# A hybrid RWKV-7 / HGRN2 layer: the input stage issued in the order of the first tile's parts, and the constants cleared by another engine

## The chip, the cores and the metric

The kernel runs on one core of one Trainium2 chip. The metric is the device time of one execution in microseconds (us), as a median of runs. The core has five engines that run side by side and meet through semaphores: TensorE (PE; its weight loads are listed apart as PEld), VectorE (DVE), ScalarE (ACT), GpSimd (POOL) and SyncE (SP), which here issues nearly all DMAs. Each engine works through its own instructions in the order in which they were issued.

## The reference

One decoder layer for two groups of tokens: 256 new tokens of one prompt, and 8 sequences of 8 tokens that continue from a stored state, 320 tokens together, D_MODEL = 2048. All is float32.

```
h = rms_norm(x, norm_g)
p = einsum('nld,dp->nlp', h, w_in)              # 2048 x 11392, one projection for everything
cur = p[..., :SHIFT_W]                          # r, k, v (1024 each), wd, ad (64 each)
sh = cur + (prev - cur) * shift_mu              # prev: the token before
w_log = -softplus(-(w0 + tanh(wd) @ w2)) - 0.5  # low-rank decay
a     = sigmoid(a0 + ad @ a2)                   # low-rank gate
y_a   = RWKV-7 recurrence, 16 heads of 64, group norm, bonus, times silu(za)
y_b   = HGRN2 recurrence, 8 heads of 128, norm, times silu(zb)
merged = sigmoid(ga) * (y_a @ proj_a) + sigmoid(gb) * (y_b @ proj_b)
y = rms_norm(x + merged @ w_out, final_norm_g)
```

The outputs are y for both groups and the new states.

## The kernel before

**Products in three parts.** A float32 operand is split in two rounded halves: `hi` (a ScalarE copy that rounds) and `lo` (the rest, by a subtraction on VectorE or GpSimd). A product is then three TensorE products, hi x hi, hi x lo and lo x hi. So a weight block of 1024 x 128 goes through four steps: a DMA of 512 KB into one of three buffers `wraw`, a copy into `whi` (ScalarE), a subtraction into `wlo`, and 24 TensorE products of 128x128 with 320 tokens. A tile of 128 output columns is two blocks. Block n uses buffer (n + 2) modulo 3.

**The input stage (lines 354 to 633).** The tokens are in three groups j: 0 and 1 are the prompt (128 tokens each), 2 is the sample (64). For each, `squares` and `scale` (ScalarE) give 1/rms, `gain` (VectorE) multiplies by it and by `norm_g` spread over all partitions (`gb`, made by four TensorE products of `sel` and `gr`, `gr` being the split `norm_g`), `turn` transposes on TensorE, `high` (ScalarE) and `low` (VectorE) split into `hhi` and `hlo`. Meanwhile `divide` splits the two blocks of the very first tile, the columns `wd` and `ad` (buffers 0 and 1), with GpSimd for the subtraction, and `first(k4)` issues its products, twelve for each quarter of the depth, all three parts of a quarter together. `warm(n)` issues n products of no use in between. Before all that GpSimd builds masks (lines 388 to 472); behind its last subtractions it clears constants (`jr_*`, `yz`, `qz`, `arp`, `lora_lw`, `lora_la`, `rs_a`, `rs_b`; lines 612 to 633). In this stage the order on each engine is the order of the program.

**The recorded stage (`record_all`, line 1318).** For eight heads, eight tiles each, then four tiles more, together with the two recurrences of a head (`rwkv`, `hgrn`). All operations are recorded first (`Recorder`); `order()` then plans them with a price for each operation, every engine free at time 0 of the plan, and issues them in the planned order: all of them therefore have the line 1376. TensorE's products of the big projection are filler: whatever else is ready goes between them. A tile's blocks are fetched in the plan too, from the third block on; the first two (buffers 2 and 0) are fetched and split in the input stage.

The first recorded work is `wd_ad`: it shifts the first tile's result (`shifted`, through `pad` and `dif`), takes tanh of its half `wd`, and puts both halves, split, into `lora_w`/`lora_lw` and `lora_a`/`lora_la`. Each is needed on both halves of the partitions, so the rounded one is copied over by GpSimd: `G.tensor_copy(dst[other], dst[own])`, line 1316. TensorE multiplies it with `wst` and `ast`, the split low-rank weights `w2a2` of the head. `bounds` computes small constants (`neg`, `lbt`).

**After it:** the gates ga and gb and the two projections (lines 1400 to 1421), then the output projection and the final norm (to line 1514).

Of the kernel before, what the change touches and what calls it, by code (L numbers as in the profile page):

```python
# [9 lines left out]
F32 = mybir.dt.float32  # L10
# [58 lines left out]
class Recorder:  # L69
# [118 lines left out]
    def order(self):  # L188

        self.link()  # L190
        free = dict.fromkeys(self.real, 0.0)
        ready = {e: [] for e in self.real}
        for o in self.ops:
            o.ready = 0.0
# [78 lines left out]
def hybrid_step(ctx, tc, x_prompt, x_sample, state_rwkv, state_hgrn, state_shift, norm_g, w_in,  # L273
# [80 lines left out]
    with tc.tile_pool(name="start", bufs=1) as st, \  # L354
# [21 lines left out]
        def divide(b_, n, sub):  # L376
            for j in range(n):
                ks = slice(8 * j // n, 8 * (j + 1) // n)
                S.copy(whi[b_][:, ks], wraw[b_][:, ks])
                sub.tensor_sub(wlo[b_][:, ks], wraw[b_][:, ks], whi[b_][:, ks].bitcast(F32))  # L380
            return whi[b_], wlo[b_]
# [95 lines left out]
        def squares(j, hf=None):  # L477
            xt, n = xts[j]
            cs = slice(0, D) if hf is None else slice(1024 * hf, 1024 * hf + 1024)
            S.activation(junk[:n, cs], xt[:n, cs], AF.Square, accum_out=ssq[j][:n, hf or 0:(hf or 0) + 1])  # L480

        def scale(j):
            n = xts[j][1]
            t_ = ssq[j][:n, 0:1]
            S.activation(t_, t_, AF.Ln, scale=1.0 / D, bias=eps_n[:n])
            S.activation(t_, t_, AF.Exp, scale=-0.5)

        def gain(j, k4, w=1):
            xt, n = xts[j]
            cs = slice(512 * k4, 512 * (k4 + w))  # L490
            V.scalar_tensor_tensor(xt[:n, cs], xt[:n, cs], ssq[j][:n, 0:1], gb[:n, cs], op0=ALU.mult, op1=ALU.mult)
# [13 lines left out]
        def high(j, k4):  # L505
            _, ks, tok = span(j, k4)
            S.copy(hhi[:, ks, tok], tps[j, k4])
# [8 lines left out]

        def warm(n):
            for _ in range(n):
                T.matmul(wps[:, :256], sel[:, 0], gr[:, :256], start=True, stop=True)

        tps = {}
        with tc.manual_schedule(engines={mybir.EngineType.PE, mybir.EngineType.Activation, mybir.EngineType.DVE,
                                        mybir.EngineType.Pool}):

            S.copy(gr[0:4], gq)
            V.tensor_sub(gr[32:36], gq, gr[0:4].bitcast(F32))
            for c_ in range(4):
                ps = pst.tile([128, 512], F32, name="gps", tag="t")
                T.matmul(ps, sel[:, c_], gr, start=True, stop=True)
                V.tensor_copy(gb[:, 512 * c_:512 * c_ + 512], ps)  # L530
            squares(2)
            scale(2)
            gain(2, 0, 2)
            turn(2, 0)
            warm(3)
            gain(2, 2, 2)
            turn(2, 1)
            warm(3)
            squares(0)
            scale(0)  # L540
            gain(0, 0, 2)
            turn(0, 0)
            turn(0, 1)
            warm(4)
            gain(0, 2, 2)
            squares(1, 0)
            squares(1, 1)
            V.tensor_add(ssq[1][:, 0:1], ssq[1][:, 0:1], ssq[1][:, 1:2])
            scale(1)
            gain(1, 0)  # L550
            turn(1, 0)
            warm(4)
            high(2, 0)
            high(0, 0)
            low(2, 0)
            low(0, 0)
            pre = [divide(0, 2, G)]
            first_ps = psm.tile([128, 512], F32, name="mps", tag="m")

            def first(k4):  # L560

                hi, lo = pre[k4 // 2]
                for w, x, last in ((hi, hhi, False), (hi, hlo, False), (lo, hhi, k4 == 3)):
                    for k_ in range(4 * k4, 4 * k4 + 4):
                        T.matmul(first_ps[:, :NT], w[:, k_ % 8], x[:, k_], start=w is hi and x is hhi and k_ == 0,
                                 stop=last and k_ == KT - 1)

            gain(1, 1)
            turn(1, 1)
            high(1, 0)  # L570
            low(1, 0)
            first(0)
            high(2, 1)
            high(0, 1)
            high(1, 1)
            gain(1, 2)
            low(2, 1)
            low(0, 1)
            low(1, 1)
            turn(0, 2)  # L580
            turn(1, 2)
            pre.append(divide(1, 2, G))
            gain(1, 3)
            first(1)
            for j in range(2):
                high(j, 2)
                low(j, 2)
            turn(0, 3)
            turn(1, 3)
            divide(2, 1, G)  # L590
            fetch(0, 0, 1)
            first(2)
            for j in range(2):
                high(j, 3)
                low(j, 3)
            ps = pst.tile([128, 512], F32, name="cps", tag="t")
            T.transpose(ps[:, :128], rows, ident)
            V.tensor_copy(cols, ps[:, :106])
            ps = pst.tile([128, 512], F32, name="sps", tag="t")
            for j in range(2):  # L600
                T.transpose(ps[:, 100 * j:100 * j + 100], ssr[:, j], ident[:100, :100])
            V.tensor_copy(sst.rearrange("p s r -> p (s r)"), ps[:, :200])
            first(3)
            divide(0, 1, G)
            for j in range(3):
                S.copy(seq4[32 * j:32 * j + 32], seqm[0:32, 0:4])
            S.copy(lvz[HS[1], :, 1], lvs[low_])
            S.copy(lvz[low_, :, 0], lvs[low_])

            jr_sum, jr_mean, jr_cent, jr_all = (ctile([128, 128], n, F32R)  # L610
                                                for n in ("jr_sum", "jr_mean", "jr_cent", "jr_all"))
            G.memset(jr_all.bitcast(F32), 1.0 / 128.0)
            for t_, x in ((jr_sum, 1.0), (jr_mean, 1.0 / 64.0)):
                G.memset(t_.bitcast(F32), 0.0)
                for sl in HS:
                    G.memset(t_[sl, sl].bitcast(F32), x)
            G.tensor_sub(jr_cent, ident, jr_mean.bitcast(F32))

            yz = ctile([128, 2, 2, 2, 64], "yz")
            yd = ctile([128, 2, 2, 64], "yd")  # L620
            qz = ctile([128, NSEQ, 32], "qz")
            arp = ctile([128, 5, 2, 2, 64], "arp")
            for t_ in (yz, qz, arp, lora_lw[HS[1]].bitcast(F32), lora_la[HS[0]].bitcast(F32)):
                G.memset(t_, 0.0)


            rs_a = ctile([128, NT], "rs_a")
            rs_b = ctile([128, NT], "rs_b")
            G.memset(rs_a, 1.0)
            G.memset(rs_a[:, 0:NP_:64], 0.0)  # L630
            G.memset(rs_a[:, NP_::8], 0.0)
            G.memset(rs_b, 1.0)
            G.memset(rs_b[:, ::8], 0.0)

    neg = ctile([128, 16], "neg")
    lbt = ctile([128, 4, 8], "lbt")
# [667 lines left out]
    def wd_ad(ps):  # L1304
        lsh = at("lsh", tag="uQ")
        shifted(24, lsh, ps)

        lo, hi = HS
        S.activation(lsh[lo], lsh[lo], AF.Exp, scale=2.0)
        S.activation(lsh[lo], lsh[lo], AF.Ln, bias=1.0)  # L1310
        S.activation(lsh[lo], lsh[lo], AF.Exp, scale=-1.0)
        V.tensor_scalar(lsh[lo], lsh[lo], -2.0, 1.0, op0=ALU.mult, op1=ALU.add)
        for dst, low, own, other in ((lora_w, lora_lw, lo, hi), (lora_a, lora_la, hi, lo)):
            S.copy(dst[own], lsh[own])
            V.tensor_sub(low[own], lsh[own], dst[own].bitcast(F32))
            G.tensor_copy(dst[other], dst[own])

    def record_all():
        io = {}
# [3 lines left out]
        def tile_of(c0, post):  # L1323
            ps = mps[ra["n"] // 2 % 2][:, :NT]
            for k8 in range(2):
                b_ = (ra["n"] + 2) % 3
                book.block = ra["n"]
                ra["n"] += 1
                raw, hi, lo = wraw[b_], whi[b_], wlo[b_]
                if ra["n"] > 2:  # L1330
                    Y.dma_start(raw, win[1024 * k8:1024 * k8 + 1024, c0:c0 + 128].rearrange("(k p) c -> p k c", p=128))
                    S.copy(hi, raw)
                    V.tensor_sub(lo, raw, hi.bitcast(F32))
                for q in range(8):
                    k = 8 * k8 + q
                    T.matmul(ps, hi[:, q, :], hhi[:, k, :], start=k == 0, stop=False)
                    T.matmul(ps, hi[:, q, :], hlo[:, k, :], start=False, stop=False)
                    T.matmul(ps, lo[:, q, :], hhi[:, k, :], start=False, stop=k == KT - 1)
            book.block = None
            post(ps)  # L1340
# [202 lines left out]
```

## Time and profile before

| | |
|---|---|
| median of 3 runs | 1167.26 us (1166.31 to 1167.61) |
| the profiled execution | 1170.25 us, its span 1168.5 us |
| TensorE busy | 1141.9 us, 98% of the span |
| VectorE busy | 777.8 us, 67% |
| ScalarE busy | 666.7 us, 57% |
| GpSimd busy | 210.6 us, 18% |
| DMA | 159.68 MB, mean 137 GB/s |

The span runs from the first to the last instruction in the trace. Busy time counts the instructions on an engine, whether they are of use or not. The page also cuts the span in 40 slices; GpSimd is busy in eight tenths of the first and in two to five tenths of those behind it, and DMA moves 168 GB/s in the first. A row of the order of time gives the start, the duration, the engine, the line, the operation, its output and inputs, and in brackets how long the engine stood idle before it and what ended the wait. A wait is put down to the last of its semaphores.

### The profile page before, as it was taken

Reading aid. Unit: us, or ns where it says so; the run is one execution under the profiler, and the core shown is the slowest. Engines: PE = TensorE matmul, PEld = TensorE weight load, DVE = VectorE, ACT = ScalarE, POOL = GpSimd, SP = SyncE. Lnnn points to the kernel's source line nnn. Section 1 sums busy time; section 2 is a strip of 40 time slices with the busy share of each in tenths; the row PEclk is TensorE's granted clock in tenths of the full one; section 3 lists DMA queues with packets and bytes.
Section 4 is the critical chain, followed back from the end, with each engine's and each line's share of the span. In section 5 each row is a group of like instructions: output and inputs, shape, how many; then the busy total and the mean of one; then the engine's idle time right before and its main releaser. Section 6 shows DMA issues by size and latency. Waiting matters only on the chain.

```text
span 1168.5 us, 20702 instructions
## 1 busy us (share of the span) xinstructions
PE 1141.9 (98%) x7775; PEld 1100.5 (94%) x7775; DVE 777.8 (67%) x1617; ACT 666.7 (57%) x1478; POOL 210.6 (18%) x429
## 2 busy tenths in 40 slices
PE   7899999999999999999999999999999999999996
PEld 6899999999999999999999999999999999988875
DVE  6778778877878888879788686444444434434542
ACT  6556766766666676667567667444444444433431
POOL 8532132122222221421321310000000000000000
PEclk9899999999999999999999999999999999999998
DMA  5643544434535435426435434555555555575632
GB/s 168 176 116 100 154 123 115 132 109 130 145 95 147 113 93 145 131 80 168 125 101 151 122 102 134 147 156 148 146 154 152 145 148 157 145 257 158 186 103 90
DMA packets 283831, 159.68 MB, mean 137 GB/s; under 512 B 22989, under 2 KB 273360, under 8 KB 283092
## 3 DMA queue, kind: packets, MB, share of 16 engines
q1 hardware_dynamic: 283220, 154.70, 47.1%
q0 software_dynamic: 512, 3.67, 1.0%
q8 instruction: 61, 1.00, 0.4%
q14 instruction: 38, 0.31, 0.1%
HBM read 148.53 MB, written 9.81 MB: 136 GB/s over the span
## 4 chain that ended last, share of the span: by engine, by line
PE 92%; DVE 3%; DMA 2%; ACT 1%; POOL 1%; issue 0%; DVEq 0%; SPq 0%; POOLq 0%; ACTq 0%
PE mps L1376 40%; PE a L1376 12%; PE mps L338 6%; PE mps L337 6%; PE mps L339 6%; PE b L1376 4%; PE po L1458 2%; PE po L1456 2%; PE po L1457 2%; DMA raw<-in_w_out_dram 2%; PE ppb L338 2%; PE ppa L338 2%; PE ppb L337 2%; PE ppa L337 2%; PE ppb L339 2%; PE ppa L339 2%
## 5 line engine op out<-in xcount | busy, mean ns | idle before, releaser
L1376 PE MATMUL mps<-hlo,whi 128*128 128x320 f32 x1088 | 345.4, 317 | 0.0
L1376 PE MATMUL mps<-hhi,whi 128*128 128x320 f32 x1088 | 345.3, 317 | 0.0
L1376 PE MATMUL mps<-hhi,wlo 128*128 128x320 f32 x1088 | 345.1, 317 | 0.0
L1376 PEld LDWEIGHTS mps<-hlo,whi 128*128 128x128 f32 x1088 | 205.4, 189 | 3.3 <-issue 3.0
L1376 PEld LDWEIGHTS mps<-hhi,wlo 128*128 128x128 f32 x1088 | 205.5, 189 | 2.7 <-issue 2.4
L1376 PEld LDWEIGHTS mps<-hhi,whi 128*128 128x128 f32 x1088 | 205.5, 189 | 0.8 <-issue 0.4
L328 DVE TENSOR_TENSOR wlo<-raw,whi 128x1024 fp32r<-128x1024 f32 x88 | 107.8, 1225 | 124.7 <-ACT whi L327 124.5
L327 ACT CAST whi<-raw 128x1024 fp32r<-128x1024 f32 x88 | 92.3, 1048 | 163.3 <-PE mps L338 107.4
L1376 ACT CAST whi<-raw 128x1024 fp32r<-128x1024 f32 x134 | 140.6, 1050 | 77.3 <-PE mps L1376 73.6
L1376 DVE TENSOR_TENSOR wlo<-raw,whi 128x1024 fp32r<-128x1024 f32 x134 | 166.7, 1244 | 24.7 <-ACT whi L1376 23.5
L337 PE MATMUL mps<-hhi,whi 128*128 128x320 f32 x448 | 138.4, 309 | 0.0
L338 PE MATMUL mps<-hlo,whi 128*128 128x320 f32 x448 | 138.4, 309 | 0.0
L339 PE MATMUL mps<-hhi,wlo 128*128 128x320 f32 x448 | 138.4, 309 | 0.0
L337 PEld LDWEIGHTS mps<-hhi,whi 128*128 128x128 f32 x448 | 84.1, 188 | 0.0
L338 PEld LDWEIGHTS mps<-hlo,whi 128*128 128x128 f32 x448 | 84.1, 188 | 0.0
L339 PEld LDWEIGHTS mps<-hhi,wlo 128*128 128x128 f32 x448 | 84.1, 188 | 0.0
L1449 DVE TENSOR_TENSOR wlo<-raw,whi 128x1024 fp32r<-128x1024 f32 x32 | 39.0, 1224 | 45.6 <-ACT whi L1448 45.5
L1448 ACT CAST whi<-raw 128x1024 fp32r<-128x1024 f32 x32 | 33.6, 1051 | 55.9 <-DMA raw<-in_w_out_dram 28.6
L1431 POOL DMA_DIRECT2D xb<-in_x_sample_dram x1 | 0.7, 721 | 341.7 <-PE mps L339 341.7
L1456 PE MATMUL po<-whi,mhi 128*128 128x512 f32 x128 | 50.7, 396 | 1.9 <-ACT whi L1448 1.2
L1458 PE MATMUL po<-wlo,mhi 128*128 128x512 f32 x128 | 50.8, 397 | 0.6 <-DVE wlo L1449 0.5
L1457 PE MATMUL po<-whi,mlo 128*128 128x512 f32 x128 | 50.5, 394 | 0.0
(410 smaller groups left out, 2344.0 us busy)
## 6 DMA issues: line engine op xcount, KB each, us to landing
raw<-in_w_in_dram SPq DMA_DIRECT2D x194, 512.0 KB
raw<-in_w_out_dram SPq DMA_DIRECT2D x32, 512.0 KB
raw<-in_proj_a_dram SPq DMA_DIRECT2D x16, 512.0 KB
raw<-in_proj_b_dram SPq DMA_DIRECT2D x16, 512.0 KB
s<-in_state_hgrn_dram SPq DMA_DIRECT2D x8, 512.0 KB
out_dram<-s SPq DMA_DIRECT2D x8, 512.0 KB
s<-in_state_rwkv_dram SPq DMA_DIRECT2D x8, 256.0 KB
out_dram<-s SPq DMA_DIRECT2D x8, 256.0 KB
```

Source lines behind the costliest of these rows:

```text
L327: S.copy(hi[:, ks], raw[:, ks])
L328: sub.tensor_sub(lo[:, ks], raw[:, ks], hi[:, ks].bitcast(F32))
L337: T.matmul(dst, hi[:, q, :], xhi[:, k, :], start=(k == 0), stop=False)
L338: T.matmul(dst, hi[:, q, :], xlo[:, k, :], start=False, stop=False)
L339: T.matmul(dst, lo[:, q, :], xhi[:, k, :], start=False, stop=(k == nk - 1))
L1376: o.fn(*o.args, **o.kw)
L1431: G.dma_start(yx[j], src)
L1448: S.copy(hi, raw)
L1449: V.tensor_sub(lo, raw, hi.bitcast(F32))
L1456: T.matmul(pt, h, hi, start=first, stop=False)
L1457: T.matmul(pt, l, hi, start=False, stop=False)
L1458: T.matmul(pt, h, lo, start=False, stop=end)
```

## The change

- **Constants.** The clears of lines 612 to 633 go from GpSimd to VectorE, to the very front of the stage, ahead of the split of `gr`; `arp` comes behind the copies of `gb`. A tile of ones, 128 x 256, is new.
- **Warming.** `warm` multiplies ones (128 partitions) instead of `sel` and `gr` (64 partitions). 16 such products are issued ahead of the first transposes; of those in between, 3 and 4 stay (before 3, 3, 4 and 4).
- **Order.** The products of the first tile are issued part by part: `first(part, k4)`, as soon as the operands of that part are there. The splits of its blocks are issued in halves (`half`) between the copies of `high`. The squares of group 1 are one instruction instead of two and an addition.
- **Second tile.** Its two blocks (buffers 1 and 2) are fetched in the input stage; the plan then begins to fetch with the fifth block.
- **Low-rank copies.** The copy to the other half of the partitions is a second ScalarE copy from `lsh` instead of one on GpSimd.
- **Plan.** The planner takes GpSimd as free from 1.7 us of the plan on.

```diff
         free = dict.fromkeys(self.real, 0.0)
+        free["G"] = 1700.0
...
         def warm(n):
             for _ in range(n):
-                T.matmul(wps[:, :256], sel[:, 0], gr[:, :256], start=True, stop=True)
+                T.matmul(wps[:, :256], ones[:, :128], ones, start=True, stop=True)
...
+            ones = st.tile([128, 256], F32R, name="ones")
+            V.memset(ones.bitcast(F32), 1.0)
+            V.memset(jr_all.bitcast(F32), 1.0 / 128.0)
+            for t_, x in ((jr_sum, 1.0), (jr_mean, 1.0 / 64.0)):
+                V.memset(t_.bitcast(F32), 0.0)
+                for sl in HS:
+                    V.memset(t_[sl, sl].bitcast(F32), x)
+            V.tensor_sub(jr_cent, ident, jr_mean.bitcast(F32))
...
+            for t_ in (yz, qz, lora_lw[HS[1]].bitcast(F32), lora_la[HS[0]].bitcast(F32)):
+                V.memset(t_, 0.0)
...
+            V.memset(rs_a, 1.0)
+            V.memset(rs_a[:, 0:NP_:64], 0.0)
+            V.memset(rs_a[:, NP_::8], 0.0)
+            V.memset(rs_b, 1.0)
+            V.memset(rs_b[:, ::8], 0.0)
             S.copy(gr[0:4], gq)
             V.tensor_sub(gr[32:36], gq, gr[0:4].bitcast(F32))
...
+            V.memset(arp, 0.0)
+            warm(16)
             squares(2)
...
-            squares(1, 0)
-            squares(1, 1)
-            V.tensor_add(ssq[1][:, 0:1], ssq[1][:, 0:1], ssq[1][:, 1:2])
+            squares(1)
...
-            pre = [divide(0, 2, G)]
...
-            def first(k4):
-                hi, lo = pre[k4 // 2]
-                for w, x, last in ((hi, hhi, False), (hi, hlo, False), (lo, hhi, k4 == 3)):
-                    for k_ in range(4 * k4, 4 * k4 + 4):
-                        T.matmul(first_ps[:, :NT], w[:, k_ % 8], x[:, k_], start=w is hi and x is hhi and k_ == 0,
-                                 stop=last and k_ == KT - 1)
+            def first(part, k4):
+                w, x = ((whi, hhi), (whi, hlo), (wlo, hhi))[part]
+                for k_ in range(4 * k4, 4 * k4 + 4):
+                    T.matmul(first_ps[:, :NT], w[k4 // 2][:, k_ % 8], x[:, k_], start=part == 0 and k_ == 0,
+                             stop=part == 2 and k_ == KT - 1)
+            def half(b_, hf):
+                ks = slice(4 * hf, 4 * hf + 4)
+                S.copy(whi[b_][:, ks], wraw[b_][:, ks])
+                G.tensor_sub(wlo[b_][:, ks], wraw[b_][:, ks], whi[b_][:, ks].bitcast(F32))
+            half(0, 0)
             high(1, 0)
             low(1, 0)
-            first(0)
+            first(0, 0)
+            gain(1, 2)
+            gain(1, 3)
+            half(0, 1)
             high(2, 1)
...
             turn(0, 2)
+            first(0, 1)
             turn(1, 2)
-            pre.append(divide(1, 2, G))
-            gain(1, 3)
-            first(1)
+            first(1, 0)
+            first(2, 0)
+            half(1, 0)
...
+            half(1, 1)
+            fetch(0, 0, 1)
...
+            first(1, 2)
+            first(2, 2)
             divide(2, 1, G)
-            fetch(0, 0, 1)
...
-            first(3)
+            for part in range(3):
+                first(part, 3)
+            fetch(1, 1024, 0)
             divide(0, 1, G)
+            fetch(2, 1024, 1)
...
-            G.memset(jr_all.bitcast(F32), 1.0 / 128.0)
...
-            G.memset(rs_b[:, ::8], 0.0)
...
             S.copy(dst[own], lsh[own])
             V.tensor_sub(low[own], lsh[own], dst[own].bitcast(F32))
-            G.tensor_copy(dst[other], dst[own])
+            S.copy(dst[other], lsh[own])
...
+                if ra["n"] > 4:
+                    Y.dma_start(raw, win[1024 * k8:1024 * k8 + 1024, c0:c0 + 128].rearrange("(k p) c -> p k c", p=128))
                 if ra["n"] > 2:
-                    Y.dma_start(raw, win[1024 * k8:1024 * k8 + 1024, c0:c0 + 128].rearrange("(k p) c -> p k c", p=128))
                     S.copy(hi, raw)
```

More of the change, by code (lines that the diff above doesn't have):

```diff
@@ L523, in hybrid_step @@
                                         mybir.EngineType.Pool}):
+            ones = st.tile([128, 256], F32R, name="ones")
+            V.memset(ones.bitcast(F32), 1.0)
+            jr_sum, jr_mean, jr_cent, jr_all = (ctile([128, 128], n, F32R)
+                                                for n in ("jr_sum", "jr_mean", "jr_cent", "jr_all"))
+            V.memset(jr_all.bitcast(F32), 1.0 / 128.0)
[4 more added lines that the diff above has]
+            V.tensor_sub(jr_cent, ident, jr_mean.bitcast(F32))
+            yz = ctile([128, 2, 2, 2, 64], "yz")
+            yd = ctile([128, 2, 2, 64], "yd")
+            qz = ctile([128, NSEQ, 32], "qz")
+            arp = ctile([128, 5, 2, 2, 64], "arp")
+            for t_ in (yz, qz, lora_lw[HS[1]].bitcast(F32), lora_la[HS[0]].bitcast(F32)):
+                V.memset(t_, 0.0)
+            rs_a = ctile([128, NT], "rs_a")
+            rs_b = ctile([128, NT], "rs_b")
+            V.memset(rs_a, 1.0)
[3 more added lines that the diff above has]
+            V.memset(rs_b[:, ::8], 0.0)
             S.copy(gr[0:4], gq)
@@ L537, in hybrid_step @@
             turn(2, 1)
-            warm(3)
+            warm(4)
             squares(0)
@@ L543, in hybrid_step @@
             turn(0, 1)
-            warm(4)
+            squares(1)
+            scale(1)
             gain(0, 2, 2)
-            squares(1, 0)
-            squares(1, 1)
-            V.tensor_add(ssq[1][:, 0:1], ssq[1][:, 0:1], ssq[1][:, 1:2])
-            scale(1)
             gain(1, 0)
             turn(1, 0)
-            warm(4)
+            gain(1, 1)
+            turn(1, 1)
             high(2, 0)
@@ L556, in hybrid_step @@
             low(0, 0)
-            pre = [divide(0, 2, G)]
             first_ps = psm.tile([128, 512], F32, name="mps", tag="m")
-            def first(k4):
-                hi, lo = pre[k4 // 2]
-                for w, x, last in ((hi, hhi, False), (hi, hlo, False), (lo, hhi, k4 == 3)):
-                    for k_ in range(4 * k4, 4 * k4 + 4):
-                        T.matmul(first_ps[:, :NT], w[:, k_ % 8], x[:, k_], start=w is hi and x is hhi and k_ == 0,
-                                 stop=last and k_ == KT - 1)
-            gain(1, 1)
-            turn(1, 1)
+            def first(part, k4):
[8 more added lines that the diff above has]
+            half(0, 0)
             high(1, 0)
             low(1, 0)
-            first(0)
+            first(0, 0)
+            gain(1, 2)
+            gain(1, 3)
+            half(0, 1)
             high(2, 1)
@@ L575, in hybrid_step @@
             high(1, 1)
-            gain(1, 2)
             low(2, 1)
@@ L580, in hybrid_step @@
             turn(0, 2)
+            first(0, 1)
             turn(1, 2)
-            pre.append(divide(1, 2, G))
-            gain(1, 3)
-            first(1)
-            for j in range(2):
-                high(j, 2)
-                low(j, 2)
+            first(1, 0)
+            first(2, 0)
+            half(1, 0)
+            high(0, 2)
+            high(1, 2)
+            low(0, 2)
+            low(1, 2)
             turn(0, 3)
             turn(1, 3)
-            divide(2, 1, G)
-            fetch(0, 0, 1)
[L592 to L595, printed above, removed]
+            first(0, 2)
+            first(1, 1)
+            first(2, 1)
+            half(1, 1)
+            fetch(0, 0, 1)
+            high(0, 3)
+            high(1, 3)
+            low(0, 3)
+            low(1, 3)
+            first(1, 2)
+            first(2, 2)
+            divide(2, 1, G)
             ps = pst.tile([128, 512], F32, name="cps", tag="t")
@@ L608, in hybrid_step @@
             S.copy(lvz[low_, :, 0], lvs[low_])
[L610 to L633, printed above, removed]
     neg = ctile([128, 16], "neg")
```

## The prediction

> **What bounds the kernel now.** I read the page's first part, then the view of what TensorE waits for (total, times, longest), then the order of time of each engine in the first 60 us, and last a table of windows.
>
> ```profile
> span 1168.5 us, 20702 instructions
> PE 1141.9 (98%) x7775; PEld 1100.5 (94%) x7775; DVE 777.8 (67%) x1617; ACT 666.7 (57%) x1478; POOL 210.6 (18%) x429
> PE a L1376 <- POOL lora_w L1376: 4.7, 1, 4.7
> PE gps L529 <- DVE gr L526: 4.4, 1, 4.4
> PE tps L503 <- DVE xt L491: 4.2, 1, 4.2
> ```
>
> TensorE is busy for 98% of the span, so the kernel is a row of matrix products and a change gains only where TensorE waits or runs slowly. Three of its waits stand out, all in the first 42 us, where the change acts. TensorE in order of time around them (start, duration), and three windows (length, busy time of TensorE, its weight loads, VectorE, ScalarE, GpSimd, then granted clock):
>
> ```profile
> 10.68 1.11 PE L503 MATMUL tps<-ident,xt 64*128 64x64 f32 x8 [4.20 <-DVE xt L491]
> ...
> 18.16 1.22 PE L519 MATMUL wps<-gr,sel 64*128 64x256 f32 x4
> ...
> 20.07 1.42 PE L565 MATMUL mps<-hhi,whi 128*128 128x320 f32 x4
> 21.29 1.17 PE L565 MATMUL mps<-hlo,whi 128*128 128x320 f32 x4
> 22.30 0.76 PE L565 MATMUL mps<-hhi,wlo 128*128 128x320 f32 x4
> 22.89 1.04 PE L503 MATMUL tps<-ident,xt 128*128 128x128 f32 x8
> ...
> 30.23 0.31 PE L1376 MATMUL mps<-hhi,whi 128*128 128x320 f32 x1
> ...
> 42.01 0.64 PE L1376 MATMUL a<-lora_w,wst 128*128 128x320 f32 x1 [4.73 <-POOL lora_w L1376]
> ```
> ```profile
> 37.28:42.01 4.73, 0.01 (x1) 0.00 (x0) 3.30 (x5) 2.24 (x3) 4.45 (x9) 0.71 0.95 230
> 42.01:46.15 4.14, 4.14 (x15) 4.14 (x16) 1.57 (x4) 2.88 (x8) 2.94 (x11) 0.51 0.75 216
> 46.15:60.00 13.85, 13.85 (x97) 13.84 (x97) 11.19 (x28) 7.59 (x18) 1.06 (x4) 1.00 0.44 122
> ```
>
> From 10.68 on TensorE waits for nothing until 37.28. The four products from 20.07 start 0.305 us apart, those from 22.30 0.147: until about 22 it works at half pace. The input stage ends at 30.23, when the planner's stream starts (call this t0). Its 48 products (blocks 0 and 1) end at 37.28; then TensorE waits 4.73 us for `lora_w`, and the wait also costs pace: the granted clock is 0.51 from 42.01 to 46.15.
>
> What makes `lora_w` late, in the same order-of-time view of GpSimd, ScalarE and VectorE (in brackets, idle time before):
>
> ```profile
> 17.04 3.04 POOL L380 TENSOR_TENSOR wlo<-raw,whi 128x512 fp32r<-128x512 f32 x2
> 30.61 0.20 POOL L612 MEMSET jr_all<- 128x128 f32 x1
> 37.52 0.16 POOL L633 MEMSET rs_b<- 128x40 f32 x1
> 40.69 1.27 POOL L1376 CAST lora_w<-lora_w 64x320 fp32r<-64x320 f32 x1
> 30.47 0.38 ACT L1376 COPY pad<-mps 128x256 f32<-128x256 f32 x1 [1.24 <-issue]
> 36.45 0.46 ACT L1376 CAST lora_w<-uQ 64x320 fp32r<-64x320 f32 x1 [1.50 <-DVE uQ L1376]
> 37.52 1.05 ACT L1376 CAST whi<-raw 128x1024 fp32r<-128x1024 f32 x1
> 38.60 1.23 DVE L1376 TENSOR_TENSOR wlo<-raw,whi 128x1024 fp32r<-128x1024 f32 x1 [0.40 <-ACT whi L1376]
> ```
>
> The chain was at ScalarE's copy by 36.91; GpSimd, held by the constants of lines 612 to 633 and clears behind them, made the second half 5.05 us later. Without it TensorE would still have waited: block 2's weights were split only at 38.57 and 39.83.
>
> **The change, step by step.**
>
> *Constants on VectorE, in front.* 18 instructions (from the row at 30.61 to that at 37.52) leave GpSimd; with `ones` added and `arp` put off, 18 now stand on VectorE ahead of the split of `gr`, and `arp` behind the copies of `gb`.
>
> ```profile
> 3.17 1.13 DVE L526 TENSOR_TENSOR gr<-gq,gr 4x512 fp32r<-4x512 f32 x1 [3.17 <-ACT gr L525]
> 5.24 2.48 DVE L530 COPY gb<-gps 128x512 f32<-128x512 f32 x4 [0.94 <-PE gps L529]
> 9.35 4.98 DVE L491 SCALAR_TENSOR_TENSOR xt<-xt,ssq,gb 64x1024 f32<-64x1024 f32 x4 [1.62 <-ACT ssq L486]
> L1509 DVE TENSOR_SCALAR xa<-xa,rs 128x512 f32<-128x512 f32 x4 | 1.9, 483 | 1.2 <-ACT rs L1503 1.2
> L1376 DVE COPY e<-uB 128x1 f32<-128x1 f32 x8 | 1.2, 145 | 0.0
> ```
>
> No VectorE clear is in this trace. The 18 cover 3,124 elements a partition. The 1024-element split (1.23 us) gives about 1.0 ns an element beyond a fixed part, the 512-element scaling (0.483) about 0.7 at most; a one-element copy takes 0.145, of which I count 0.06, as the next one overlaps it. Upper end 3.1 + 18 x 0.06 = 4.2 us; lower end half the first term, 2.6. From 0.8 us, when engines start, that is 5.0 or 3.4, against 3.17: `gr` is 1.8 or 0.2 late. `gb` ends at 7.72 now, so at 9.5 or 7.9; `arp` adds 1.3 or 0.8. The gain starts at 9.35 now, for ScalarE's sum of squares; then at 10.8 or 9.35. I take 10.8, the one-element pace being nearest to an operation without a second read. The Trainium skill (VectorE: DVE Perf Modes, "Zero memsets can be issued as uint32 (trn2)") says a memset takes one cycle per element whatever the type, an estimate of 3.3 us at its 0.96 GHz, which speaks for the upper end; no run here shows it yet.
>
> *Input stage in a new order.* Its work, in the view that groups by line and shape (count, busy us, mean ns):
>
> ```profile
> L491 DVE SCALAR_TENSOR_TENSOR xt<-xt,ssq,gb 128x512 f32<-128x512 f32 x4 | 3.8, 952 | 0.6 <-ACT ssq L486 0.6
> L511 DVE TENSOR_TENSOR hlo<-tps,hhi 128x512 fp32r<-128x512 f32 x10 | 6.4, 681 | 3.2 <-ACT hhi L507 3.2
> L380 POOL TENSOR_TENSOR wlo<-raw,whi 128x512 fp32r<-128x512 f32 x4 | 6.0, 1524 | 1.7 <-ACT whi L379 1.6
> L380 POOL TENSOR_TENSOR wlo<-raw,whi 128x1024 fp32r<-128x1024 f32 x2 | 4.8, 2394 | 1.3 <-ACT whi L379 1.3
> ```
>
> Today TensorE sets its end: half pace to 22, and each group of twelve products queued behind transposes and warming. With 16 full-height warming products in TensorE's 4.2 us hole and groups issued part by part, VectorE sets it: from 10.8, gains 4.98 + 3.8 and lows 6.4 make 26.0; the last two parts behind the last low cost 2 x 0.59 (22.30 to 22.89), so 27.2, and 0.2 for hand-overs: t0 = 27.4, or 2.8 earlier. Ends: 25.9 with cheap clears, 29.4 if half pace stays through six parts (six times 0.305 x 4 against 0.59 adds 3.8, of which TensorE's waits for VectorE hide about half). The warming products cost nothing: 16 at 1.22 / 4 = 0.31 us are 4.9, behind the `gb` products at about 8.3, so to 13.2; the first transposes, ready at 12.1, come 1.1 late, but VectorE's gains don't wait for them and its first low stands only at 17.4. If it did, up to 1.1 would be lost. The one addition on VectorE and the halved squares that go (0.2 us) are inside this. GpSimd's splits, 6.0 + 4.8 from 17.04, end at 27.9 at best; block 0 needs the one before the last at about 25.5 and block 1 the last 3.5 us after t0: covered, with under 0.5 us to spare on the first.
>
> *Low-rank copies on ScalarE.* The chain from ScalarE's first `pad` copy (30.47) to the end of the `lora_w` cast (36.91) is 6.44 us. It now ends in a second ScalarE cast (0.46, as the first) instead of GpSimd's. Against it: block 2's split (1.23) now stands ready early on VectorE, and is likely planned ahead of the chain; GpSimd's copy into `pad` waits for the last split, on which the planner's 1.7 us start for GpSimd bears. So `lora_w` at t0 + 0.24 + 6.44 + 0.46 + 1.23 = t0 + 8.4. The stream covers 7.05 (30.23 to 37.28). Wait left: 1.3 instead of 4.73, a gain of 3.4. Ends: 0, if the plan puts the products behind part of block 2, and 3.3, if VectorE's early scalings are held as now (the 16-column one, below).
>
> *Clock.* From 42.01 to 46.15 TensorE did 16 products of the long kind's pace, 4.14 us; at 0.147 they are 2.35. A wait of 1.3 should not bring the clock down: 1.8 gained. The windows bear this out only for 4.73 us, in which a mean of 0.71 means the clock held about 2 us before it halved.
>
> *Prefetch of blocks 2 and 3.* Two 512 KB loads move from behind SP's `w2a` and state loads to ahead of them, and wait for the raw buffers.
>
> ```profile
> 29.26 0.48 SPq L1376 DMA_DIRECT2D w2a<-in_rwkv_w_dram  x1
> 28.93 2.05 DVE L1376 TENSOR_SCALAR neg<-cols 128x16 f32<-128x16 f32 x1
> 46.74 0.60 PE L1376 MATMUL a<-ident,s 128*128 128x128 f32 x4
> ```
>
> Their last buffer comes free near 26 to 27, so SP reaches `w2a` by about 28, at t0 + 0.5, where it now stands at t0 - 1.0; its reader, a ScalarE cast, stands just ahead of the `whi` row at 37.52, 8 us behind, and the states are read at 46.74: nothing lost; with that slack gone, the move would cost 1.5. Weights ready at t0 + 7 are what lets the wait fall at all; counted there.
>
> Sum: 2.8 + 3.4 + 1.8 = 8.0. The profiled execution took 1170.25 us around a span of 1168.5; the median, 1167.26, lies 3.0 below. 1167.3 - 8.0 = 1159.3.
>
> **The rivals.**
>
> *The front stays at half pace.* Half pace held from 10.68 to 22 although TensorE was never idle, mostly with transposes; after the 16 products come transposes again. Then t0 is about 28.6 (1.6 gained), but GpSimd and VectorE are further ahead, so the wait falls to about 0.5: 1.6 + 4.2 + 1.8 = 7.6, less up to 1 for products still slow: 1160.5. The Trainium skill (TensorE: Matmul & The Clock Gate, "Part 4: PE-mode transpose") says transposes do not count as activity for the clock; the trace agrees so far (0.305 us at 20.07).
>
> *All hidden.* Cheap clears (t0 26.0) and no wait: 4.2 + 4.7 + 1.8 = 10.7: 1156.6. For it: each end is open. Against: GpSimd's splits.
>
> *The change doesn't remove the wait.* VectorE's 16-column scaling took 2.05 us beside GpSimd's split; if it and block 2's split delay the chain by 3 us, the wait is 3.3 or more and the clock falls again: 2.8 + 1.4 + 0.3 = 4.5: 1162.8.
>
> *Slower: the new plan.* The recorded 700 us are planned anew from another start. One group of products stands once in each head, in the chain of work in order of time (first, the two farthest apart, last of eight):
>
> ```profile
> 69.66 2.16 PE a L1376 x10
> 318.53 2.16 PE a L1376 x10
> 403.19 2.16 PE a L1376 x10
> 647.77 2.16 PE a L1376 x10
> ```
>
> (647.77 - 69.66) / 7 = 82.6; the longest, 318.53 to 403.19, is 84.7. Were all eight like it, 2.1 x 8 = 17 us would be lost: 1176. From 1.0 us a head it eats the gain. Against it: TensorE is full there whatever the order.
>
> **How the numbers follow.** Sum as worked 0.46, slow front 0.17, all hidden 0.14, wait stays 0.13, slower plan 0.06, the rest spread. Range 1155.5 to 1164.0: from beyond "all hidden" to above "wait stays". A change under 0.2% (2.3 us) can't be told from none: faster means below 1164.9: 0.89; same 0.05; slower 0.06.
>
> **What would show it.** Right: `lora_w` written by ScalarE alone, under 2 us of wait before its product, 1.00 granted behind it, the first product of the stream at 26.5 to 28.5, the first gain near 10.8. Wrong: products 0.3 us apart after 20 us; a TensorE wait above 3 us; heads over 83.6 us apart.

## The result

| | before | changed |
|---|---|---|
| median of 6 runs | 1167.03 us (1166.31 to 1168.04) | 1161.04 us (1160.13 to 1162.17) |
| the profiled execution, its span | 1170.25 us, 1168.5 | 1162.17 us, 1160.4 |
| input stage ends (t0) | 30.23 | 29.14 |
| wait for the low-rank operands | 4.73 | 0.75 |
| granted clock behind it | 0.51 over 4.1 us | 1.00 |
| first head's mark / eighth head's | 69.66 / 647.77 | 63.18 / 640.23 |

The changed kernel is faster by 6.0 us: ratio 0.9948, 95% interval 0.9936 to 0.9961. Forecast were 8.0 us and 1159.3.

TensorE in the changed kernel, in order of time (start, duration, in brackets the idle time before and what ended it):

```profile
12.52 0.91 PE L504 MATMUL tps<-ident,xt 64*128 64x64 f32 x8
...
18.14 0.86 PE L591 MATMUL mps<-hhi,whi 128*128 128x320 f32 x4
18.83 0.60 PE L504 MATMUL tps<-ident,xt 128*128 128x128 f32 x4
...
20.11 0.86 PE L591 MATMUL mps<-hhi,whi 128*128 128x320 f32 x4 [0.68 <-ACT hhi L508]
...
22.58 0.86 PE L591 MATMUL mps<-hhi,wlo 128*128 128x320 f32 x4 [0.58 <-POOL wlo L598]
...
29.14 0.31 PE L1396 MATMUL mps<-hhi,whi 128*128 128x320 f32 x1
...
38.12 0.39 PE L1396 MATMUL a<-lora_a,ast 128*128 128x320 f32 x1 [0.75 <-DVE ast L1396]
```

The same engine in windows (length; busy time of TensorE, its weight loads, VectorE, ScalarE, GpSimd; granted clock; share and GB/s of the DMA engines):

```profile
34.00:40.00 6.00, 5.25 (x36) 5.01 (x36) 4.61 (x11) 5.40 (x13) 4.68 (x15) 1.00 1.19 293
40.00:46.00 6.00, 6.00 (x44) 6.00 (x43) 4.70 (x10) 4.87 (x13) 1.71 (x7) 1.00 0.64 170
```

The 4.73 us wait has become 0.75, and the clock stays at 1.00. What came last is now `ast`, the split weights; the product with `lora_w`, which ScalarE writes alone, runs at 39.38 without a wait. The stage ends only 1.1 us earlier. The other engines show why; the order of time of VectorE, GpSimd and ScalarE:

```profile
0.94 0.27 DVE L526 MEMSET ones<- 128x256 f32 x1 [0.94 <-PEq L1551]
2.53 0.69 DVE L535 TENSOR_TENSOR jr_cent<-ident,jr_mean 128x128 fp32r<-128x128 f32 x1
5.94 0.68 DVE L554 TENSOR_TENSOR gr<-gq,gr 4x512 fp32r<-4x512 f32 x1
10.27 1.12 DVE L559 MEMSET arp<- 128x1280 f32 x1 [0.22 <-issue]
11.31 6.14 DVE L492 SCALAR_TENSOR_TENSOR xt<-xt,ssq,gb 64x1024 f32<-64x1024 f32 x6
```
```profile
10.12 6.79 POOL L453 TENSOR_TENSOR mk<-mk,seqm 128x64 f32<-128x64 f32 x2
21.24 5.03 POOL L598 TENSOR_TENSOR wlo<-raw,whi 128x512 fp32r<-128x512 f32 x4
29.20 2.41 POOL L381 TENSOR_TENSOR wlo<-raw,whi 128x1024 fp32r<-128x1024 f32 x1 [0.56 <-ACT whi L380]
31.54 0.21 POOL L1396 COPY pad<-sst 128x8 f32<-128x8 f32 x1
```
```profile
28.07 1.05 ACT L380 CAST whi<-raw 128x1024 fp32r<-128x1024 f32 x1 [2.14 <-DMA raw<-in_w_in_dram]
30.22 0.37 ACT L1396 COPY pad<-mps 128x256 f32<-128x256 f32 x1
38.33 0.46 ACT L1396 CAST lora_w<-uQ 64x320 fp32r<-64x320 f32 x1
```

The clears hold VectorE from 0.94 to 5.94, so the first gain starts at 11.31. VectorE's six gains run from 11.31 to 17.4. Two GpSimd products of masks that begin just ahead of them take 6.79 us, the first alone 6.09 (2.38 for both before). GpSimd begins its splits at 21.24 instead of 17.04, and TensorE waits for one of them at 22.58.

Where the 8.1 us between the two spans are, by the mark that stands once in each head (first and eighth, in the chain of work in order of time, changed kernel):

```profile
63.18 2.16 PE a L1396 x10
640.23 2.16 PE a L1396 x10
```

At the first mark 6.5 us are gained: 1.1 from t0, 4.0 from the wait, the other 1.4 from the pace (between t0 and the mark TensorE is busy for 33.29 us instead of 34.70). From first to eighth mark the new plan takes 577.05 instead of 578.11, 1.1 less; the rest of the span 520.2 instead of 520.7. The medians differ by only 6.0: the profiled execution of before lies 3.2 above its median, that of the changed kernel 1.1. The second profile of before (below) tells in which places.

### The profile page after: what moved, and what is told of

Same layout as the page of the kernel before. It is cut to its first block, busy times and chain, and to the rows that moved or that the text cites. A ratio compares the mean times of both kernels' runs of the same rounds, so it can differ in the third digit from the quotient of the medians.

```text
span 1160.4 us, 20721 instructions
## 1 busy us (share of the span) xinstructions
PE 1137.6 (98%) x7784; PEld 1095.8 (94%) x7784; DVE 778.6 (67%) x1635; ACT 667.3 (58%) x1478; POOL 210.1 (18%) x409
## 4 chain that ended last, share of the span: by engine, by line
PE 91%; DVE 2%; DMA 2%; POOL 2%; ACT 1%; issue 0%; DVEq 0%; POOLq 0%; ACTq 0%; SPq 0%
PE mps L1396 40%; PE a L1396 12%; PE mps L340 6%; PE mps L338 6%; PE mps L339 6%; PE b L1396 4%; DMA raw<-in_w_out_dram 2%; PE po L1478 2%; PE po L1476 2%; PE po L1477 2%; PE ppb L340 2%; PE ppa L340 2%; PE ppa L338 2%; PE ppb L338 2%; PE ppb L339 2%; PE ppa L339 2%
```

## The experiments

Three theories stood. **1:** at the first stall two things were late, GpSimd's low-rank copy and block 2's weights; both must go. **2:** one of them alone made it. **3:** the gain is the input stage. Each kernel's median of 5 to 12 runs stands beside the kernel before on the same chip, at 1167.8 to 1168.3 us. The changed kernel stood beside a median of 1167.0. Its variants are therefore compared with it by their ratios to before (its own is 0.9948, 0.9936 to 0.9961), and 1 us between two medians is not told apart.

| kernel | median us (range) | t0 | waits behind it | mark 1 | span |
|---|---|---|---|---|---|
| before, again | 1168.3 (1163.8 to 1170.9) | 31.03 | 3.42 | 68.66 | 1166.5 |
| before + ScalarE copy | 1166.0 (1163.1 to 1167.6) | 31.09 | 0.91 + 0.71 | 67.62 | 1164.2 |
| before + clears in front | 1167.0 (1165.2 to 1168.7) | 32.42 | 0.26 + 0.84 + 0.70 | 69.06 | 1165.5 |
| before + prefetch | 1166.8 (1165.6 to 1169.3) | 31.30 | 0.68 + 1.78 | 67.32 | 1164.1 |
| before + prefetch + ScalarE copy | 1161.6 (1160.7 to 1163.1) | 30.34 | none | 63.69 | 1158.9 |
| changed, no prefetch | 1168.1 (1164.4 to 1170.7) | 29.14 | 1.53 + 1.34 + 0.36 | 68.97 | 1167.4 |
| changed, copies on GpSimd | 1162.1 (1161.8 to 1164.4) | 29.15 | 0.49 + 0.85 | 64.12 | 1160.4 |
| changed, plan from 0 | 1163.8 (1162.5 to 1164.1) | 29.18 | 1.91 | 64.38 | 1161.9 |
| changed, no 16 products | 1161.8 (1161.0 to 1162.5) | 30.16 | none | 63.44 | 1160.3 |
| changed, masks first | 1161.1 (1160.9 to 1161.3) | 30.18 | none | 63.44 | 1159.6 |
| changed, clears spread | 1159.8 (1159.5 to 1161.4) | 26.55 | 1.55 | 61.37 | 1158.1 |
| same, later plan | 1159.7 (1158.2 to 1160.1) | 28.48 | none | 61.52 | 1158.4 |

The waits are TensorE's longest between t0 and mark 1. One sum orders the numbers: mark 1 = t0 + 33.3 + waits + what half pace costs. Without a wait 33.3 is what remains (63.44 - 30.18 = 33.26; 33.0 with the later plan). The last term is a remainder and not a measurement of its own.

### The kernel before, a second time

> The kernel before, unaltered, profiled a second time. The first profiled execution had a span of 1168.5 us and a time 3.0 us above the median; the changed kernel's profile is within 1.1 us of its own. Theory 1 (part of the cost behind the 4.73 us wait is chance: the slow clock behind it lasts until the next clock window ends, so it varies from execution to execution): span 1165 to 1166, the input stage and the wait of the same lengths within 0.3 us, the slow stretch behind the wait 1 to 2.5 us shorter, or the slow clock at the end of the span gone. Rival (the planned stage takes a different time in each execution): the heads' distances differ.

TensorE in its order of time, and the windows of the wait and behind it:

```profile
31.03 0.31 PE L1376 MATMUL mps<-hhi,whi 128*128 128x320 f32 x1
41.51 0.63 PE L1376 MATMUL a<-lora_w,wst 128*128 128x320 f32 x1 [3.42 <-POOL lora_w L1376]
```
```profile
38.09:41.51 3.42, 0.00 (x0) 0.00 (x0) 2.06 (x4) 2.02 (x3) 3.14 (x8) 0.93 1.12 265
41.51:45.70 4.19, 4.19 (x19) 4.19 (x20) 2.84 (x5) 3.14 (x9) 2.93 (x11) 0.65 0.60 168
```

Partly as expected. The span is 1166.5, the slow stretch shorter (0.65 on average instead of 0.51). But stage and wait are not of the same lengths: t0 is 0.8 later and the wait 1.3 shorter, since `lora_w` came at about the same moment. The heads' distances are equal (first to eighth mark 578.11 both times); the second half of the 2 us between the two spans lies behind the eighth mark. So a microsecond of t0 means nothing while another chain sets when the wait ends.

### One edit to the kernel before: the copy on ScalarE

```diff
-            G.tensor_copy(dst[other], dst[own])
+            S.copy(dst[other], lsh[own])
```

> The kernel before with one edit: the copy of the low-rank inputs to the other half of the partitions is a ScalarE copy. Theory 1 (two things were late for the first planned stall, GpSimd's copy and block 2's weights, which stood ready at 39.83 us): the 4.73 us wait shrinks but does not go; the low-rank products start near 38, TensorE then waits for block 2's weights until 39 to 40, in sum about 2.3 us, so 2.4 us are gained, and up to 1.8 more if the shorter waits leave the clock at full rate: 1162.8 to 1164.6. Theory 2 (GpSimd's copy alone was late): no wait over 1 us is left, 1161.0 or less, as the changed kernel. Theory 3 (the gain is the input stage's order): no change, 1167.

TensorE behind t0, and windows:

```profile
39.05 0.39 PE L1376 MATMUL a<-lora_w,wst 128*128 128x320 f32 x1 [0.91 <-DVE wst L1376]
41.29 0.60 PE L1376 MATMUL mps<-hhi,wlo 128*128 128x320 f32 x1 [0.71 <-DVE wlo L1376]
```
```profile
38.00:42.00 4.00, 2.38 (x11) 1.75 (x11) 2.33 (x5) 3.21 (x7) 3.88 (x14) 0.92 1.02 242
42.00:46.00 4.00, 4.00 (x21) 3.96 (x21) 3.93 (x7) 4.00 (x12) 0.93 (x5) 0.65 0.71 203
```

Ratio 0.9982 (0.9971 to 0.9994), about 2 us: theory 1's picture, a shorter wait and then one for block 2's weights, but 1.4 us above its range of times: two waits of 1.6 us together still brought the clock down (0.65 from 42 to 46).

### One edit to the kernel before: the clears on VectorE in front

```diff
-            G.memset(jr_all.bitcast(F32), 1.0 / 128.0)
...
+            V.memset(jr_all.bitcast(F32), 1.0 / 128.0)
...
             S.copy(gr[0:4], gq)
...
+            V.memset(arp, 0.0)
             squares(2)
```

> The kernel before with one edit: the constants are cleared by VectorE in front of the stage (the large one behind the copies of the norm weights), as in the changed kernel; the low-rank copy stays on GpSimd. Theory 1: the first gain starts near 11.3 us instead of 9.35 as in the changed kernel's trace, so the input stage ends 1 to 2 us later than 30.2; GpSimd is free for the low-rank copy, and the wait is then set by block 2's weights, about 1 to 2 us; with the clock held that is 3 to 5 us gained less 1 to 2 lost: 1163 to 1165. Theory 2 (GpSimd's constants alone made the wait, and VectorE's front is free): 1161. Theory 3 (the low-rank copy must leave GpSimd): 1167 or more.

Ratio 0.9997 (0.9985 to 1.0008): nothing gained, less than theory 1 asked. t0 is 2.2 later than in the kernel's first profile and 1.4 later than in its second, the waits sum to 1.8, and the clock fell all the same (0.58 from 42 to 46). The time is that of theory 3 there, but not for its reason: TensorE waited for split weights (0.26, 0.84, 0.70) and not for GpSimd's copy.

### One edit to the kernel before: the early loads

```diff
             first(3)
+            fetch(1, 1024, 0)
             divide(0, 1, G)
+            fetch(2, 1024, 1)
...
-                if ra["n"] > 2:
+                if ra["n"] > 4:
                     Y.dma_start(raw, ...)
+                if ra["n"] > 2:
```

> The kernel before with one edit: the two early loads of the second tile. Theory 1 (two things were late, GpSimd's low-rank copy behind its constants and block 2's weights, and either alone keeps the wait): the copy of lora_w still comes at 41 to 42 us; TensorE now has products of block 2 in front of it, up to seven of the plan's, and then waits 2.5 to 3.5 us; the clock falls as before: 1166 to 1168 beside 1168 of the kernel before. Theory 2 (the loads alone were the gain, as their removal from the changed kernel cost 7 us): 1161 to 1162.5.

GpSimd in order of time, and TensorE:

```profile
38.74 0.67 POOL L1379 CAST lora_a<-lora_a 64x320 fp32r<-64x320 f32 x1
42.18 0.45 POOL L1379 CAST lora_w<-lora_w 64x320 fp32r<-64x320 f32 x1
```
```profile
39.47 0.41 PE L1379 MATMUL a<-lora_a,ast 128*128 128x320 f32 x1 [0.68 <-POOL lora_a L1379]
42.68 0.41 PE L1379 MATMUL a<-lora_w,wst 128*128 128x320 f32 x1 [1.78 <-POOL lora_w L1379]
```

Ratio 0.9996 (0.9984 to 1.0007). Theory 1: with the weights there, GpSimd's copy still ends at 42.6 and TensorE stands in front of it. The clock, expected to fall, stayed at 1.00 in this profile. Theory 2 is out for the loads.

### Two edits to the kernel before: the early loads and the copy on ScalarE

Both diffs above together; clears, order and warming products as before.

> The kernel before with two edits: the early loads of the second tile and the low-rank copies on ScalarE; constants, order and warming stay. Theory 1: both late things are gone; low-rank products near 38.5 us with a wait under 1 us, clock at 1.00 behind it, first head's mark near 64 to 65 (the stage still ends at 30.2 to 31.1): 1161.5 to 1163. Theory 3 (the input stage's order and the clears off GpSimd matter as much): a wait of 2 us or more, or 1165 and above.

TensorE, its windows, and GpSimd at that time:

```profile
30.34 0.31 PE L1379 MATMUL mps<-hhi,whi 128*128 128x320 f32 x1
38.60 0.39 PE L1379 MATMUL a<-lora_w,wst 128*128 128x320 f32 x1
```
```profile
36.00:40.00 4.00, 3.97 (x27) 3.70 (x26) 2.80 (x5) 3.88 (x10) 3.88 (x17) 1.00 0.99 234
40.00:46.00 6.00, 6.00 (x44) 5.99 (x43) 5.83 (x17) 4.78 (x13) 3.05 (x12) 1.00 0.56 160
```
```profile
34.06 1.17 POOL L626 MEMSET arp<- 128x1280 f32 x1
38.65 0.17 POOL L635 MEMSET rs_b<- 128x40 f32 x1
```

1161.56 us, ratio 0.9948 (0.9932 to 0.9964): the whole gain of the change with two of its edits. GpSimd still clears constants until 38.8, and TensorE waits for none of it. Theory 3 is out.

### The changed kernel without the early loads

> The changed kernel without the two early loads of the second tile: the plan fetches blocks 2 and 3 again. Theory 1: their loads stand behind the low-rank weights and the states, issued at about 33 us, so the weights are split at 38 to 39, while TensorE has used up blocks 0 and 1 at 36.2: a wait of 2 to 3 us, 1163 to 1164.5. Rival (the loads were hidden anyway): within 0.5 us of 1161.0.

TensorE and ScalarE in order of time, and windows:

```profile
37.88 0.42 PE L1394 MATMUL a<-lora_w,wst 128*128 128x320 f32 x1 [1.53 <-DVE lora_lw L1394]
40.42 0.63 PE L1394 MATMUL mps<-hhi,whi 128*128 128x320 f32 x1 [1.34 <-ACT whi L1394]
```
```profile
39.32 1.04 ACT L1394 CAST whi<-raw 128x1024 fp32r<-128x1024 f32 x1 [1.18 <-DMA raw<-in_w_in_dram]
```
```profile
36.00:42.00 6.00, 2.68 (x10) 1.50 (x9) 3.14 (x5) 3.22 (x6) 1.25 (x4) 0.86 1.07 258
42.00:48.00 6.00, 6.00 (x27) 5.96 (x27) 5.55 (x13) 5.74 (x16) 1.13 (x5) 0.57 0.65 183
```

Ratio to before 1.0 (0.9989 to 1.0012): the whole gain is gone, twice what was expected. The waits, 3.2 in sum, are of the size expected; half pace behind them adds 3.3 at mark 1 (68.97 - 29.14 - 33.3 - 3.2).

### The changed kernel with the copies on GpSimd

> The changed kernel with the low-rank copies back on GpSimd. Theory 1: GpSimd no longer has the constants, but still has the clears of the recorded stage in its queue; the copies then come 0.5 to 1.5 us later than ScalarE's, hidden in part behind block 2's products, which are there by now: 0 to 1 us lost, 1161 to 1162. Rival (the copy on ScalarE is what removed the wait): a wait of 3 us or more comes back, 1164 or more.

```profile
35.36 0.45 POOL L1396 CAST lora_a<-lora_a 64x320 fp32r<-64x320 f32 x1 [1.21 <-ACT lora_a L1396]
37.51 0.77 POOL L1396 CAST lora_w<-lora_w 64x320 fp32r<-64x320 f32 x1 [0.73 <-ACT lora_w L1396]
```

In GpSimd's order of time both copies wait for ScalarE, not for GpSimd. 1162.1 us: three runs within 0.4 and two 2.3 above; the ratio, 0.9963 (0.9949 to 0.9978), overlaps that of the changed kernel. With the constants off GpSimd, the copy need not leave it; either of the two edits frees `lora_w`.

### The plan's start, the warming products, the masks

Three single edits to the changed kernel: `free["G"]` back to 0, `warm(16)` left out, and the 32-wide masks built behind the masks that are multiplied.

> The changed kernel with GpSimd free at 0 of the plan again. Theory 1 (the planned start matters by where it puts the low-rank products in TensorE's order): they stand earlier in the order than they are ready, so the wait grows from 0.75 to between 1 and 2 us and the clock falls in part of the executions: 1161.3 to 1163.5, with a wider spread. Rival (the plan's start changes nothing that is not hidden): within 0.3 us of 1161.0.

> The changed kernel without the 16 warming products in front. Theory 1 (they bring the clock up, and the transposes behind them do not lower it): without them products of the first tile start 0.3 us apart until about 22 us, and the stage ends 1 to 2 us later than 29.14: 1162 to 1163. Rival (the pace there comes from elsewhere, or TensorE waits for VectorE anyway): within 0.4 us of 1161.0.

> The changed kernel with GpSimd's masks in another order: the two products of the masks, which took 6.79 us against 2.38 before as they ran beside VectorE's gains, are made ahead of the 32-wide masks. Theory 1 (the two engines shut each other out while both read two operands): the products take about 2.4 us again, GpSimd reaches its first split at about 17 instead of 21.2 us, TensorE's wait of 0.6 us for it goes and the stage ends 0.6 to 1.3 us earlier: 1159.7 to 1160.5. Rival (GpSimd's lateness is hidden): within 0.3 us of 1161.0.

*Plan from 0:* the largest wait in the planned stage becomes

```profile
PE a L1395 <- DVE wst L1395: 1.9, 1, 1.9
```

and the median 1163.8, by the ratio to before (0.9962, 0.9947 to 0.9976) about 1.6 above the changed kernel, with overlapping intervals. The span of the profile is 1.5 longer; 1.2 of it stands at mark 1, from the wait. *No 16 products:* 1161.8, ratio 0.9940: not told apart from the changed kernel; t0 is 30.16, the wait is gone instead. *Masks first:* 1161.1, ratio 0.9935, not told apart either. Its expectation failed in an instructive way: the two products, now early, took 0.55 us, but GpSimd's next mask was held in their place.

```profile
10.62 5.53 POOL L416 TENSOR_SCALAR_AFFINE_SELECT mf<-mf 64x64 f32<-64x64 f32 x1
12.52 1.11 PE L504 MATMUL tps<-ident,xt 64*128 64x64 f32 x8
20.00 1.34 PE L591 MATMUL mps<-hhi,whi 128*128 128x320 f32 x4
```

That operation took 1.22 us before. And here, behind the same 16 products, TensorE's first products of the tile still run at half pace (four in 1.34), where the changed kernel's profile had full pace at 18.14 and the one without the 16 products at 20.00 (four in 0.86): the products do not fix the pace.

### A faster version: the clears in VectorE's holes

```diff
-            V.tensor_sub(jr_cent, ident, jr_mean.bitcast(F32))
...
             V.tensor_sub(gr[32:36], gq, gr[0:4].bitcast(F32))
+            for t_ in (yz, qz):
+                V.memset(t_, 0.0)
...
-            V.memset(arp, 0.0)
+            for t_ in (lora_lw[HS[1]].bitcast(F32), lora_la[HS[0]].bitcast(F32)):
+                V.memset(t_, 0.0)
+            V.memset(rs_a, 1.0)
             warm(16)
...
             divide(2, 1, G)
+            V.memset(arp, 0.0)
+            V.memset(rs_a[:, 0:NP_:64], 0.0)
+            V.memset(rs_a[:, NP_::8], 0.0)
+            V.memset(rs_b, 1.0)
+            V.memset(rs_b[:, ::8], 0.0)
+            V.tensor_sub(jr_cent, ident, jr_mean.bitcast(F32))
```

> The changed kernel with the same VectorE clears, spread over the holes VectorE has: the four matrix constants in front, two behind the split of the norm weights, three behind the copies of the norm weights, the others behind the last low part. Theory 1 (the clears in front of the split delay the whole input stage): the split of the norm weights is done near 3.8 instead of 6.6 us, the first gain starts near 9.4 to 9.8 instead of 11.3, the input stage ends 1 to 2 us earlier than 29.14: 1159 to 1160. Rival (the end is set by GpSimd's late splits, not by the clears): the gain is earlier but the stage's end moves by less than 0.5 us: 1160.6 to 1161.2.

> The changed kernel with the clears spread over VectorE's holes (1159.8 by itself, with a wait of 1.55 us for the low-rank weights) and GpSimd planned as free from 3.5 us on. Theory 1 (TensorE's wait is the plan putting the low-rank products ahead of their operands): they stand 11 products or 1.6 us later in the order, the wait goes, the clock is safe, all executions within 1 us: 1158.0 to 1159.0. Rival (the chain behind the low-rank products is itself on the path, so a later place only moves the wait to the products behind): 1159.5 to 1160.5.

VectorE and TensorE of the first of the two:

```profile
3.21 1.09 DVE L543 TENSOR_TENSOR gr<-gq,gr 4x512 fp32r<-4x512 f32 x1 [0.79 <-ACT gr L542]
9.11 6.55 DVE L492 SCALAR_TENSOR_TENSOR xt<-xt,ssq,gb 64x1024 f32<-64x1024 f32 x6
```
```profile
26.55 0.31 PE L1395 MATMUL mps<-hhi,whi 128*128 128x320 f32 x1
36.33 0.39 PE L1395 MATMUL a<-lora_a,ast 128*128 128x320 f32 x1 [1.55 <-DVE ast L1395]
```

The gain starts at 9.11 and t0 comes 2.6 earlier; the wait takes 0.8 back. 1159.8 us, ratio to before 0.9927 (0.9914 to 0.9939), the changed kernel's being 0.9948 (0.9936 to 0.9961). With a later plan the wait goes, as theory 1 had it, but t0 was 28.48 in that profile (TensorE's pace again: eight transposes in 1.11) and the time is the same, 1159.7 (ratio 0.9926, 0.9912 to 0.9940): not the 1158 to 1159 expected. Both lie below the changed kernel, by 1.2 and 1.4 us in the medians and by 2.4 and 2.6 by the ratios; the intervals overlap a little.

## Why the prediction was right, and where not

The time lies in the range and on the forecast side, and the forecast of the mechanism holds: `lora_w` late behind GpSimd's constants, block 2's weights late as well ("without it TensorE would still have waited"), both removed, clock held. Of the signs named for it, the first product of the stream missed: 29.14 instead of 26.5 to 28.5. Point by point:

- **Input stage, forecast 2.8, measured 1.1.** This is the term that was mis-sized. VectorE's part came out near its sum: its last low part ended at 25.8, forecast 26.0. But TensorE still had five groups of four products to do then, not two: "VectorE sets it" was wrong, TensorE's queue in order did, held at 20.11 and 22.58. The row that should have warned is GpSimd's 2.38 us for two mask products beside VectorE's gains, which take 0.55 away from them; the sum let GpSimd's splits start at 17.04 as before, and they started at 21.24. And the 1.1 seem to hang on the pace: in the two profiles of the changed kernel's order whose transposes took 1.11 (masks first, no 16 products), t0 was 30.18 and 30.16, against 30.23 and 31.03 for the kernel before. The rival of a slow front had put 28.6 there.
- **What t0 is worth.** The sum added t0 and the wait as independent terms. They are not: with t0 at 30.18 or 30.16 the wait is zero and mark 1 the same within 0.3. The low-rank chain starts with GpSimd's copy into `pad`, behind its last split (31.54 in the changed kernel, 31.02 with two edits alone), and with ScalarE's, behind a cast that waits for a load (28.07). The step named the first of these and still hung the chain on t0.
- **The wait, forecast 1.3 left, measured 0.75,** and for `ast`, not for `lora_w`; the plan put the first low-rank product behind seven products of block 2. That end of the range was named.
- **The clock, forecast 1.8, measured about 1.4 at mark 1,** with an unsafe reason: "A wait of 1.3 should not bring the clock down". 0.91 + 0.71 did, in one execution; 1.91 in one piece and 0.68 + 1.78 did not, in others. (The 16 products of that sum are 15 in its window.)
- **The clears, forecast 5.0 for the split of `gr`, measured 5.94;** one 128 x 128 subtraction took 0.69 beside GpSimd, and gaps stand between the clears. The largest clear, 1280 elements, took 1.12 us. By the Trainium skill's rule (VectorE: DVE Perf Modes, "Zero memsets can be issued as uint32 (trn2)"), a cycle per element, it would be an estimate of 1.33 us at that page's 0.96 GHz; the trace has a sixth less.
- **The new plan** did no harm: 577.05 from first to eighth mark, 1.1 less.
- **From span to median.** The span came out as forecast, 1160.4 against 1160.5, by luck: 1.1 + 4.0 + 1.4 = 6.5 instead of 8.0, and 1.6 behind the first mark that no term had. The median lies 1.7 above. The step "3.0 below" carried the offset of before's profile over to the changed kernel; its own offset is 1.1.

What stays open: how much idle time lowers the clock. Single times of the kernel before lie between 1163.1 and 1172.3, those of the kernel with masks first between 1160.9 and 1161.3; that the clock makes this spread is argued from two profiles, not shown. Open too is what sets TensorE's pace in the input stage.

## What to carry to other kernels

When an engine stands before a late operand, ask what it would do next and whether that is there: here either edit alone brought 0 to 2 us and the two together 6, as much as the whole change. A stage that ends earlier gains only if the chain behind it starts with the stage; find what the chain's first instruction stands behind in its own queue. Work moved to an idle engine goes into its holes, not in front of its critical work.

## What the runs showed of the hardware that was not expected

GpSimd's two products of masks in three profiles (kernel before; masks first; clears spread):

```profile
10.87 2.38 POOL L452 TENSOR_TENSOR mk<-mk,seqm 128x64 f32<-128x64 f32 x2
7.21 0.55 POOL L444 TENSOR_TENSOR mk<-mk,seqm 128x64 f32<-128x64 f32 x2
11.85 2.40 POOL L453 TENSOR_TENSOR mk<-mk,seqm 128x64 f32<-128x64 f32 x2
```

Away from the gains the two take 0.55 us. Begun under running gains, which read two operands from SBUF, they take 2.4, about one gain (1.3) each, also when six gains run one behind another (9.11 to 15.7). But an operation that began beside the clear of `arp`, just ahead of the gains, was held for three or four of them: 6.09 us in the changed kernel, 5.53 with masks first, 4.88 without the 16 products, 4.66 in before with the clears in front. The Trainium skill (SBUF — State Buffer, "Who interferes with whom") has the contention of such a VectorE operation with GpSimd's reads, and the traces agree; why the hold is one gain in some places and several in others is not shown. And the pace of TensorE in the first 20 us differs between executions of the same instructions: behind the same 16 products, eight transposes took 0.91 us in one profile and 1.11 in another, at a granted clock of 1.00 in both.
